# A two-layer RWKV-7 and Conformer backbone on one core: latent chains get PSUM banks, state and tiles of their own, and the next pair's chain is written right behind its merge

## The chip, the cores and the metric

The kernel runs on one core of a Trainium2 chip. The metric is the device time of one execution in microseconds (us); lower is better.

## What is computed

The input is a stream of 512 latent tokens and a prefix of 256 context tokens, each of width 1024. The first layer (below) runs an RWKV-7 mixer in both directions over context and latents, with 16 heads of 64, beside a gated short convolution; both go through one output projection. The second layer is a Conformer convolution on the latents alone.

```python
def wkv_scan(S0, r, decay, k, v, kk, a, reverse):
    def step(S, inp):
        sa = jnp.einsum("bhvk,bhk->bhv", S, -kk_t)
        S = (S * w_t[:, :, None, :] + sa[..., None] * (kk_t * a_t)[:, :, None, :]
             + v_t[..., None] * k_t[:, :, None, :])
        return S, jnp.einsum("bhvk,bhk->bhv", S, r_t)
...
    yac, S_f, S_b = rwkv_seq(rwkv_prep(hc, rc, kc, vc, *rw), zero, zero, ...)
    ya, _, _ = rwkv_seq(rwkv_prep(h, r, k, v, *rw), S_f, S_b, r_k, lnx_w, lnx_b, True)
    yb = bg * dwconv(cg * xb, sc_w, seg_len)
    y = jnp.concatenate([ya * jax.nn.silu(za), yb * jax.nn.silu(zb)], axis=-1) @ w_out
```

## The kernel before

**Tiling.** The recurrence is taken in chunks of 64 tokens (4 of the context, 8 of the latents) and in 8 pairs of heads. A pair's work falls into steps: `prep_lat`, `light` and `heavy` make the products within the chunks (AR, BK, and E, the masked matrices); `solve` inverts the triangular blocks on VectorE, with a transpose of Nt into X (L737) and 31 times a product (xtmp, L743) and a sum (Y, L745); `merge` joins the inverted blocks and writes them into E; the chain then goes over the chunks in sequence. `finish` normalises a pair's outputs and turns them (po), and `conv_branch` makes the short convolution of the same columns, with four projections in the order cg, xb, bg, zb; the last of them (tile pzb) gates its result.

**The chain.** `chain_lat(st, i)` is one of 8 steps, forward and backward direction (z = 0, 1) at once. A step is a line of dependent pieces: matmuls of the state H and of earlier values into zo; ScalarE copies the sum to Zs (L865); matmuls with E into uh; ScalarE copies them to UV (L872); matmuls with BKt into the same bank uh; VectorE makes the new state Hl from it (L879); ScalarE scales it for the next step (HPl, L833). The step's outputs collect in bank on (tile onl) and are evicted at the step's end, by ScalarE in steps 0 to 3 (L888) and by an addition on VectorE in steps 4 to 7 (L891), into tile O. PSUM tiles zo, on, po and the merge's mg rotate over three banks (`ps_zo`: two with tag zo, and uh1); uh of all chains is one bank.

**The order.** Each engine takes its instructions in its own queue, in order. The queues are laid out when the program is built: a list scheduler takes what is ready by its planned times, and among these what was written first. The written order is the loop over 12 stages (from L1049): stages 0 to 3 run the context chains, 4 to 11 the chains of latent pairs 0 to 7. A latent stage writes its own chain, and then by the letters of `STAGE[2]` ("OSPLMHFC"): O (po of the next stage), S (solve of the next), P and L (prep and light of the one after), M (merge of the next), H (heavy of the one after), F (projection fills, and finish of its own), C (conv_branch, one pair behind the chain's count: stage 10 writes convolution 7 and stage 11 only the last chain and its finish).

**The end of the layer.** Behind convolution 7 the pool of the right side is closed and the out-projection's pool opened in its space, so the loads of wr (the rows of w_out) and yr wait until the last gate projection has read its operands. `outproj` makes 384 matmuls (tiles o) for the first half of the tokens: for each of 16 row blocks, ScalarE casts wr to wh and VectorE subtracts to wl (`hilo`), and three products each are taken. Block 8 has its weights in early tiles (we8h, we8l). The matmuls of out-projection stand behind chain 7 in the written order.

## Time and profile before

| | us |
|---|---|
| median of 3 runs | 1387.38 (1385.10 to 1389.39) |
| profiled execution, its time | 1384.0 |
| profiled execution, its span | 1382.2 |
| TensorE matmuls, busy | 1319.8 (95%) |
| VectorE, busy | 986.4 (71%) |
| ScalarE, busy | 744.4 (54%) |
| clock granted to TensorE, mean share | 0.992 |

The span is the time from the first to the last instruction of the profile. In profile lines PE is TensorE's matmuls, PEld its weight loads (which overlap them), DVE VectorE, ACT ScalarE, POOL GpSimd, and SPq the queue from which SyncE issues transfers. Starts and durations are in us from the span's start; `x` counts instructions, and `<-` in square brackets names what ended a wait. Tiles are named by the program, with their numbers left out: Hl is the state of a latent chain, ARl a latent AR.

| in the profile of before | us |
|---|---|
| first latent chain's state update | from 484.5 |
| last latent chain's first matmul | 871.4 |
| last latent chain's last output | 901.9 |
| layer 1's first out-projection matmul | 872.0 |

### The profile page before, as it was taken

To read this page: it belongs to the slowest core of one execution; us is meant where nothing else is said; L and a number is where in the kernel's file an instruction comes from. 1 tells how busy PE (TensorE), PEld (TensorE's weight loads), DVE (VectorE), ACT (ScalarE), POOL (GpSimd) and SP (SyncE) were. 2 spreads that over 40 slices of the span, in tenths; PEclk is the share of its full clock that TensorE was granted. 3 is DMA by queue.
4 is the path that set the end of the run, shared out by engine and by line. 5 is a ranking of instruction groups with operands and counts; after the bars stand their busy time and mean duration, and the time that the engine had idled before them with its cause. 6 is when DMAs were issued, how large, how long until landed. Compare 5 with 4: busy or idle time off the path is not lost.

```text
span 1382.2 us, 29703 instructions
## 1 busy us (share of the span) xinstructions
PE 1319.8 (95%) x11925; PEld 975.1 (71%) x11925; DVE 986.4 (71%) x2304; ACT 744.4 (54%) x1509; POOL 127.7 (9%) x263
## 2 busy tenths in 40 slices
PE   6999999999998999999999989999999999999998
PEld 2657777777666766666666666677777787788886
DVE  5857879867999499999999998458653653644323
ACT  6546476555765476675756755547742432554222
POOL 4142200001101010101101000010000000000000
PEclk9999999999999999999999999999999999999999
DMA  9865522222323322223222221578621321133232
GB/s 334 272 215 198 161 62 75 92 75 77 96 86 88 97 76 73 78 66 86 77 72 78 76 72 48 187 264 284 203 70 53 122 74 49 62 116 98 92 99 84
DMA packets 139754, 158.54 MB, mean 115 GB/s; under 512 B 15503, under 2 KB 104223, under 8 KB 139497
## 3 DMA queue, kind: packets, MB, share of 16 engines
q1 hardware_dynamic: 123152, 106.47, 24.9%
q0 software_dynamic: 15856, 49.12, 10.9%
q8 instruction: 93, 1.52, 0.5%
q10 hardware_dynamic: 608, 1.06, 0.2%
q14 instruction: 45, 0.37, 0.1%
HBM read 138.33 MB, written 18.28 MB: 113 GB/s over the span
## 4 chain that ended last, share of the span: by engine, by line
PE 46%; DVE 12%; ACT 7%; issue 4%; DMA 4%; POOL 0%; SPq 0%; DVEq 0%; ACTq 0%; POOLq 0%
PE pu L57 12%; PE pz L57 6%; PE f L57 6%; PE pxb L57 3%; PE pcg L57 3%; PE uh L57 3%; PE o L57 2%; DVE E L686 2%; DMA wr<-in_ev_w_out_dram 2%; PE pzb L57 1%; PE zol L57 1%; PE onl L57 1%; PE px L57 1%; PE pc L57 1%; DVE Yl L745 1%
## 5 line engine op out<-in xcount | busy, mean ns | idle before, releaser
L57 PE MATMUL o<-wh,y 128*128 128x512 f32 x248 | 79.8, 396 | 0.0
L743 DVE TENSOR_TENSOR xtmpl<-Xl,Yl 128x126 f32<-128x126 f32 (+22 forms) x248 | 62.3, 251 | 3.1
L745 DVE TENSOR_TENSOR Yl<-Yl,xtmpl 128x126 f32<-128x126 f32 (+22 forms) x248 | 62.2, 251 | 2.9
L1281 ACT CAST ah<-a 64x512 fp32r<-64x512 f32 x32 | 19.8, 618 | 74.8 <-DVE a L1276 74.4
L57 PEld LDWEIGHTS uh<-UV,BKt 128*64 128x64 f32 x704 | 26.4, 136 | 37.6 <-ACT UV L872 27.8
L57 PEld LDWEIGHTS o<-wh,y 128*128 128x128 f32 x248 | 46.2, 188 | 9.5
L57 PE MATMUL pal<-ARl,BKl 64*128 64x128 f32 x512 | 44.5, 295 | 8.7 <-DVE E L686 7.3
L57 PE MATMUL o<-wl,y 128*128 128x512 f32 x124 | 49.7, 401 | 2.3 <-DVE wl L130 2.3
L872 ACT COPY UV<-uh 64x128 f32<-64x128 f32 x128 | 33.3, 260 | 28.9 <-PE uh L57 26.6
L57 PEld LDWEIGHTS pal<-ARl,BKl 64*128 64x128 f32 x512 | 35.3, 191 | 18.8 <-issue 11.1
L130 DVE TENSOR_TENSOR wl<-wr,wh 128x1024 fp32r<-128x1024 f32 x28 | 34.2, 1223 | 19.1 <-ACT wh L129 19.0
L1276 DVE TENSOR_TENSOR a<-pu,a 128x512 f32<-128x512 f32 x16 | 11.0, 691 | 50.0 <-PE pu L57 47.7
L57 PE MATMUL uh<-UV,BKt 128*64 128x64 f32 x704 | 36.5, 232 | 8.7 <-ACT UV L872 4.5
L686 DVE TENSOR_TENSOR E<-pal,maskE 128x512 f32<-128x512 f32 x64 | 42.9, 684 | 0.3
L1233 DVE SCALAR_TENSOR_TENSOR pr<-px,dbe,What 119x512 f32<-119x512 f32 x32 | 22.6, 746 | 26.6 <-PE px L57 26.6
L129 ACT CAST wh<-wr 128x1024 fp32r<-128x1024 f32 x28 | 29.6, 1056 | 19.3 <-DMA wr<-in_ev_w_out_dram 10.1
L57 PEld LDWEIGHTS uh<-Ol,E 64*64 64x64 f32 x512 | 20.3, 133 | 25.8 <-ACT Ol L865 23.6
L879 DVE SCALAR_TENSOR_TENSOR Hl<-uh,PCl,HPl 128x64 f32<-128x64 f32 x112 | 26.2, 276 | 13.7 <-PE uh L57 5.2
L833 ACT ACTIVATE HPl<-Hl,PCl 128x64 f32<-128x64 f32 x96 | 28.1, 340 | 11.0 <-DVE Hl L879 9.8
L745 DVE TENSOR_TENSOR Yc<-Yc,xtmpc 128x126 f32<-128x126 f32 (+22 forms) x124 | 31.5, 254 | 3.1
L743 DVE TENSOR_TENSOR xtmpc<-Xc,Yc 128x126 f32<-128x126 f32 (+22 forms) x124 | 31.5, 254 | 3.0
L57 PEld LDWEIGHTS zol<-Hl,ARl 64*64 64x64 f32 x448 | 18.0, 134 | 21.0 <-DVE xtmpl L743 5.4
(1002 smaller groups left out, 4284.1 us busy)
## 6 DMA issues: line engine op xcount, KB each, us to landing
wr<-in_ev_w_out_dram SPq DMA_DIRECT2D x28, 512.0 KB, 5.2
mwr<-in_mod_w_dram POOLq DMA_DIRECT2D x28, 256.0 KB, 4.2
wrv<-in_ev_w_in_dram SPq DMA_DIRECT2D x16, 256.0 KB, 2.9
ectx<-in_mod_w_dram POOLq DMA_DIRECT2D x16, 256.0 KB, 4.4
wrr<-in_ev_w_in_dram SPq DMA_DIRECT2D x16, 256.0 KB, 2.9
wrza<-in_ev_w_in_dram SPq DMA_DIRECT2D x16, 256.0 KB, 2.8
wrcg<-in_ev_w_in_dram SPq DMA_DIRECT2D x16, 256.0 KB, 2.9
wrxb<-in_ev_w_in_dram SPq DMA_DIRECT2D x16, 256.0 KB, 2.9
```

The source lines that it names most:

```text
L57: env["pe"] = T.matmul(o, lhsT, rhs, start=start, stop=stop)
L129: S.copy(hi, raw)
L130: env["lo"].tensor_tensor(out=lo, in0=raw, in1=hi, op=ALU.subtract)
L686: st["ev"].append(V.tensor_tensor(out=E[:, h, z * NLAT + c0 : z * NLAT + c0 + m, :], in0=pas[h], in1=maskE[:, z * (1 + h) : z * (1 + h) + ...
L743: V.tensor_tensor(out=tv, in0=X[:, :i, i : i + 1].to_broadcast([P, i, m]), in1=Y[:, i : i + 1, c0:].to_broadcast([P, i, m]), op=ALU.mult)
L745: V.tensor_tensor(out=Y[:, :i, c0:], in0=Y[:, :i, c0:], in1=tv, op=ALU.add)
L833: S.activation(t[:, z, :], H[:, z, :], AF.Copy, scale=st["PC"][z][:, i : i + 1])
L872: u_ = S.copy(UV[ZR[1 - h], i : 2 * nch - i : 2 * nch - 1 - 2 * i, ZR[h]], uh[ZR[1 - h], 0:2, :])
L879: h_ = V.scalar_tensor_tensor(out=Hn[:, z, :], in0=uh[:, 2 + z, :], scalar=PC[z][:, i : i + 1], in1=HP[:, z, :], op0=ALU.mult, op1=ALU.add)
L1233: V.scalar_tensor_tensor(out=pr[s][:NPROD], in0=px[s][:NPROD], scalar=dbe[:, 0:1], in1=What[:, n * 512 : n * 512 + 512], op0=ALU.add, op1= ...
L1276: V.tensor_tensor(out=a, in0=pp[1], in1=a, op=ALU.mult)
L1281: S.copy(ahl[s][hr], a[hr])
```

## The change

Every latent chain gets two banks by its pair's parity: X (uh0 or uh1) for the sums that were in zo, and Y (one of the two zo tiles, now named zy0 and zy1) for uh, the state update and the outputs. H and HP are halves of fixed tiles. The two directions' AR lie in one tile, and Zs and the outputs overwrite the chunks of AR that are used up, so the tile O goes. A step's outputs are no longer computed and evicted in the step itself: `outs(i, H)` keeps them, and step i+1 takes the first four matmuls between its own, the other four behind its copy Zs, and then evicts, ahead of its matmuls into Y. `merge` of a latent pair writes into solve's tiles X and Y from pair 1 on. `finish` turns the outputs in the pair's bank Y. In the written order, only stage 4 writes its own chain; a latent stage writes the next pair's chain (new letter X) right behind the next pair's merge.

```diff
-STAGE = ("KLSMVHvF", "OPLSMHF", "OSPLMHFC")
+STAGE = ("KLSMVHvF", "OPLSMHF", "OSMXPLHFC")
...
-    def ps_zo(name):
-        flip["zo"] = (flip["zo"] + 1) % 3
-        return ps.tile([P, 512], F32, tag="uh1" if flip["zo"] == 2 else "zo", name=name, bufs=1 if flip["zo"] == 2 else 2)
...
-    NBUF = {"tmp": 3, "bon": 3, "AR": 6, "BK": 2, "BKt": 4, "UV": 2, "E": 2, "PC0": 4, "PC1": 4, "rnq": 2,
+    NBUF = {"tmp": 3, "bon": 3, "AR": 3, "BK": 2, "BKt": 4, "UV": 2, "E": 2, "PC0": 4, "PC1": 4, "rnq": 2,
...
+        if st["lat"] and st["p"]:
+            Xt, Yt = st["XY"]
+            R1, R2, Gs = (t.rearrange("p (a b) -> p a b", b=32) for t in (Xt[:, 0:512], Xt[:, 512:], Yt))
...
-        pg = px = ps_zo("mg" + nm)
+        pg = px = uhs[1 - st["p"] % 2] if st["lat"] else uhs[1]
...
         if i == 0:
+            par = p % 2
+            if not lat2:
+                lat2["y"] = [ps.tile([P, 512], F32, tag="zo", name=f"zy{x}", bufs=2) for x in range(2)]
+                lat2["h"] = [w(t, f"{t}l{x}") for x, t in enumerate(("H", "H", "HP"))]
+            st["py"] = lat2["y"][par]
+            st["xy"] = ch3(uhs[1 - par]), ch3(lat2["y"][par])
+            *st["hn"], st["hp"] = [t[:, par * P : par * P + P].rearrange("p (z x) -> p z x", z=2) for t in lat2["h"]]
             st["HP"] = scale_H(st, st["H"], 0)
-            st["O"] = ch3(w("O", f"O{nm}"))
+            st["go"] = pinned()
...
+        def outs(i, H):
+            cs = (i, nch - 1 - i)
+            oc = (4, 5) if i < nch // 2 else (5, 4)
+            first = [(lambda h=h, z=z: go(Y[ZR[h], oc[z], :], AR[z][ZR[h], cs[z], CH:], H[ZR[h], z, :], z == 1, False))
+                     for z in (1, 0) for h in (1, 0)]
+            then = [(lambda h=h, z=z: go(Y[ZR[h], oc[z], :], E[:, h, z * nch + cs[z], CH:],
+                                         UV[:, z * nch + cs[z], ZR[h]], False, z == 1)) for h, z in hz]
+
+            def evict():
+                if i < nch // 2:
+                    S.copy(Q[:, 2 * i + 1 : 32 - 2 * i : 30 - 4 * i, :], Y[:, 4:6, :])
+                else:
+                    o = Q[:, 15 - 2 * i : 18 + 2 * i : 2 + 4 * i, :]
+                    V.tensor_tensor(out=o, in0=Y[:, 4:6, :], in1=o, op=ALU.add)
+
+            return first, then, evict
...
-        zo, on = st["zo"], ch3(ps_zo(f"on{nm}_{i}"))
+        first, then, evict = st.get("outs") or ([], [], lambda: None)
         for z in (1, 0):
             for h in range(2):
-                m0_ = cmm(zo[ZR[1 - h], z, :], AR[z][ZR[h], cs[z], 0:CH], H[ZR[h], z, :], False, z == 0)
-                cmm(on[ZR[1 - h], oc[z], :], AR[z][ZR[1 - h], cs[z], CH:], H[ZR[1 - h], z, :], z == 1, False)
+                m0_ = go(X[ZR[1 - h], z, :], AR[z][ZR[h], cs[z], 0:CH], H[ZR[h], z, :], False, z == 0)
+                if first:
+                    first.pop(0)()
...
-        S.copy(Zs, zo[:, 0:2, :])
+        Zs = Q[:, 2 * i : 31 - 2 * i : 30 - 4 * i, :]
+        S.copy(Zs, X[:, 0:2, :])
+        closing([], then, evict)
         ahead = values(i + 1) if i < nch - 1 else []
         for h, z in hz:
-            cmm(uh[ZR[1 - h], z, :], E[ZR[1 - h], h, z * nch + cs[z], 0:CH], Zs[ZR[1 - h], z, :])
+            go(Y[ZR[1 - h], z, :], E[ZR[1 - h], h, z * nch + cs[z], 0:CH], Zs[ZR[1 - h], z, :])
...
+        st["outs"] = outs(i, H)
...
-        else:
+        elif s == 4:
             for i in range(NLAT):
                 chain_lat(st, i)
...
+            elif x == "X":
+                for i in range(NLAT):
+                    chain_lat(sts[s + 1], i)
```

What this moves in the queues is shown at three places.

**TensorE at the end of convolution 7.** pzb7 is the gate projection of the last convolution; o01 and its like are out-projection. Before, the last pzb7 rows and the first step of chain 7 (zol7, onl7) read:

```order
L57 MATMUL pzb7_10982<-hlh1_447,whzb71_10977 128x512
L57 MATMUL pzb7_10982<-hll1_448,whzb71_10977 128x512
L57 MATMUL pzb7_10982<-hlh1_447,wlzb71_10978 128x512
L57 MATMUL zol7_0_11021<-UV110_4903,E110_4904 64x64 x4
L57 MATMUL zol7_0_11021<-h0_7_9897,ARl71_9989 64x64
L57 MATMUL onl7_0_11026<-h0_7_9897,ARl71_9989 64x64
L57 MATMUL zol7_0_11021<-h0_7_9897,ARl71_9989 64x64
L57 MATMUL onl7_0_11026<-h0_7_9897,ARl71_9989 64x64
L57 MATMUL zol7_0_11021<-h0_7_9897,ARl70_9959 64x64
L57 MATMUL onl7_0_11026<-h0_7_9897,ARl70_9959 64x64
L57 MATMUL zol7_0_11021<-h0_7_9897,ARl70_9959 64x64
L57 MATMUL onl7_0_11026<-h0_7_9897,ARl70_9959 64x64
L57 MATMUL o01_11335<-we8h_11340,ye8_11338 128x512
L57 MATMUL o01_11335<-we8l_11341,ye8_11338 128x512
```

After, uh0 and zy1 are chain 7's banks X and Y, and these are the last pzb7 rows and the rest of that step's matmuls up to the first row of out-projection:

```order
L57 MATMUL zy1_5340<-UV110_4884,E110_4885 64x64 x4
L57 MATMUL pzb7_10958<-hlh1_443,whzb71_10953 128x512
L57 MATMUL pzb7_10958<-hll1_444,whzb71_10953 128x512
L57 MATMUL pzb7_10958<-hlh1_443,wlzb71_10954 128x512
L57 MATMUL zy1_5340<-ARl7_10051,E110_4885 64x64
L57 MATMUL uh0_125<-UV110_4884,E110_4885 64x64
L57 MATMUL zy1_5340<-ARl7_10051,E110_4885 64x64
L57 MATMUL uh0_125<-UV110_4884,E110_4885 64x64
L57 MATMUL zy1_5340<-ARl7_10051,E110_4885 64x64
L57 MATMUL uh0_125<-UV110_4884,E110_4885 64x64
L57 MATMUL zy1_5340<-ARl7_10051,E110_4885 64x64
L57 MATMUL uh0_125<-UV110_4884,E110_4885 64x64
L57 MATMUL o01_11031<-we8_11036,ye8_11034 128x512 x2
```

The last pzb7 stood ahead of the first matmul of chain 7 and stands now in its sixth step (step 5); out-projection began in the first step and begins now in the sixth.

**VectorE around the start of solve 7.** The transpose into Xl7 is solve 7's first instruction; orq5 and bonl5 belong to the finish of pair 5 and yb6 to convolution 6. Before:

```order
L954 TENSOR_TENSOR yb6_10302<-pbg6_10318,yb6_10302 128x512
L502 TENSOR_TENSOR orq5_10188<-orq5_10188 128x8
L130 TENSOR_TENSOR wlcg70_10853<-wrcg70_10851,whcg70_10852 128x512
L503 TENSOR_TENSOR orq5_10188<-orq5_10188 128x8
L504 SCALAR_TENSOR_TENSOR orq5_10188<-orq5_10188 128x8
L911 TENSOR_TENSOR Ol5_9551<-Ol5_9551,orq5_10188 128x512
L686 TENSOR_TENSOR E110_4904<-pal7000_10110,maskE_107 128x512
L686 TENSOR_TENSOR E110_4904<-pal7001_10111,maskE_107 128x512
L920 SCALAR_TENSOR_TENSOR bonl5_8260<-po5_10203,hcol_77,bonl5_8260 128x512
L921 SCALAR_TENSOR_TENSOR bonl5_8260<-bonl5_8260,hcol_77,gz5_10220 128x512
L737 STREAM_TRANSPOSE Xl7_10668<-Nt_111 128x32x32
L743 TENSOR_TENSOR xtmpl7_10670<-Xl7_10668,Yl7_10669 128x31
```

After, at the same place, with Hl0, the first state update of chain 6:

```order
L942 TENSOR_TENSOR ARl5_8449<-ARl5_8449,orq5_10201 128x2x4x64
L915 SCALAR_TENSOR_TENSOR Hl0_5341<-zy0_5339,PCl60_9243,HPl2_5343 128x64
L915 SCALAR_TENSOR_TENSOR Hl0_5341<-zy0_5339,PCl61_9272,HPl2_5343 128x64
L737 STREAM_TRANSPOSE Xl7_10401<-Nt_111 128x32x32
L743 TENSOR_TENSOR xtmpl7_10403<-Xl7_10401,Yl7_10402 128x31
L745 TENSOR_TENSOR Yl7_10402<-Yl7_10402,xtmpl7_10403 128x31
L743 TENSOR_TENSOR xtmpl7_10403<-Xl7_10401,Yl7_10402 128x30
```

and a few rows on:

```order
L915 SCALAR_TENSOR_TENSOR Hl1_5342<-zy0_5339,PCl60_9243,HPl2_5343 128x64
L915 SCALAR_TENSOR_TENSOR Hl1_5342<-zy0_5339,PCl61_9272,HPl2_5343 128x64
L951 SCALAR_TENSOR_TENSOR bonl5_8426<-zy1_5340,hcol_77,bonl5_8426 128x512
L743 TENSOR_TENSOR xtmpl7_10403<-Xl7_10401,Yl7_10402 128x81
L952 SCALAR_TENSOR_TENSOR bonl5_8426<-bonl5_8426,hcol_77,gz5_10232 128x512
L745 TENSOR_TENSOR Yl7_10402<-Yl7_10402,xtmpl7_10403 128x27x3
L743 TENSOR_TENSOR xtmpl7_10403<-Xl7_10401,Yl7_10402 128x78
L745 TENSOR_TENSOR Yl7_10402<-Yl7_10402,xtmpl7_10403 128x26x3
L130 TENSOR_TENSOR we8_11036<-wre8_11037,we8_11036 128x1024
L985 TENSOR_TENSOR yb6_10314<-pbg6_10330,yb6_10314 128x512
```

The first update of chain 6 stood 22 rows behind the transpose of solve 7 and stands now just ahead of it; bonl5 and yb6, which stood ahead, now stand among the solve's operations.

**ScalarE where out-projection's first weights are cast.** y0_9 and wh0_9 are the casts of the first block of yr and wr; UV110 is the chain's copy. Before, from the last cast of convolution 7's weights into the second step of chain 7:

```order
L129 CAST whzb71_10977<-wrzb71_10976 128x512 [waits DMAHW7_49,PE_49]
L898 ACTIVATE gzb7_11007<-pzb7_10982 128x512 [waits PE_49]
L865 COPY Ol7_11020<-zol7_0_11021 128x128 [waits DVE_49,PE_49,Activation_49]
L872 COPY UV110_4903<-uh0_125 64x2x64 [waits PE_49]
L872 COPY UV110_4903<-uh0_125 64x2x64
L129 CAST y0_9_11361<-yr0_9_11362 128x256 [waits DMAHW0_49]
L888 COPY Ol7_11020<-onl7_0_11026 128x2x64 [waits PE_49]
L833 ACTIVATE HPl7_1_11054<-Hl7_0_11051,PCl70_9952 128x64 [waits DVE_49]
L833 ACTIVATE HPl7_1_11054<-Hl7_0_11051,PCl71_9981 128x64
L865 COPY Ol7_11020<-zol7_1_11036 128x128 [waits PE_49]
L129 CAST wh0_9_11367<-wr0_9_11366 128x1024 [waits DMAHW1_49]
L872 COPY UV110_4903<-uh0_125 64x2x64 [waits PE_49]
```

After, from the Zs copy of step 5 (ARl7) of chain 7:

```order
L899 COPY ARl7_10051<-uh0_125 128x2x64 [waits PE_49]
L929 ACTIVATE gzb7_10983<-pzb7_10958 128x512 [waits PE_49]
L907 COPY UV110_4884<-zy1_5340 64x2x64 [waits DVE_49,PE_49]
L907 COPY UV110_4884<-zy1_5340 64x2x64
L837 ACTIVATE HPl2_5343<-Hl1_5342,PCl70_10044 128x64 [waits DVE_49]
L837 ACTIVATE HPl2_5343<-Hl1_5342,PCl71_10073 128x64 [waits DVE_49,Activation_49]
L129 CAST y0_9_11056<-yr0_9_11057 128x256 [waits DMAHW0_49]
L899 COPY ARl7_10051<-uh0_125 128x2x64 [waits PE_49]
L129 CAST wh0_9_11062<-wr0_9_11061 128x1024 [waits DMAHW1_49]
L907 COPY UV110_4884<-zy1_5340 64x2x64 [waits DVE_49,PE_49]
```

The cast wh0_9 stood ahead of the UV copies of step 1 and stands now ahead of those of step 6; the gate gzb7 stood ahead of the chain and stands in its step 5.

More of the change, by code (lines that the diff above doesn't have):

```diff
@@ L161 @@
     l0, rs = ExitStack(), ExitStack()
-    flip = {"mm": 0, "at": 0, "zo": 0}
+    flip = {"mm": 0, "at": 0}
     I32 = mybir.dt.int32
@@ L249, in start @@
         dft = w("xtmp", "dft")[:31, :NPROD]
-        tokt = [w("AR", f"tok{j}") for j in range(6)]
+        tokt = [t[:, D * j : D * j + D] for t in [w("AR", f"tok{j}") for j in range(3)] for j in range(2)]
         for j in range(6):
@@ L855, in chain_lat, with closing @@
+        def closing(first, then, evict):
+            for f in first + then:
+                f()
+            evict()
         if i == 0:
-            for go in values(0):
-                go()
-        zo, on = st["zo"], ch3(ps_zo(f"on{nm}_{i}"))
+            for f in values(0):
+                f()
+        first, then, evict = st.get("outs") or ([], [], lambda: None)
         for z in (1, 0):
             for h in range(2):
-                m0_ = cmm(zo[ZR[1 - h], z, :], AR[z][ZR[h], cs[z], 0:CH], H[ZR[h], z, :], False, z == 0)
-                cmm(on[ZR[1 - h], oc[z], :], AR[z][ZR[1 - h], cs[z], CH:], H[ZR[1 - h], z, :], z == 1, False)
+                m0_ = go(X[ZR[1 - h], z, :], AR[z][ZR[h], cs[z], 0:CH], H[ZR[h], z, :], False, z == 0)
+                if first:
+                    first.pop(0)()
@@ L871, in chain_lat @@
         for h in range(2):
-            u_ = S.copy(UV[ZR[1 - h], i : 2 * nch - i : 2 * nch - 1 - 2 * i, ZR[h]], uh[ZR[1 - h], 0:2, :])
+            u_ = S.copy(UV[ZR[1 - h], i : 2 * nch - i : 2 * nch - 1 - 2 * i, ZR[h]], Y[ZR[1 - h], 0:2, :])
         h_ = None
+        st["outs"] = outs(i, H)
         if i < nch - 1:
             for h, z in hz[::-1]:
-                cmm(uh[ZR[h], 2 + z, :], BKt[z][:, cs[z], ZR[h]], UV[:, z * nch + cs[z], ZR[h]])
-            Hn = w("H", f"H{nm}_{i}")[:, 0:P].rearrange("p (z x) -> p z x", z=2)
+                go(Y[ZR[h], 2 + z, :], BKt[z][:, cs[z], ZR[h]], UV[:, z * nch + cs[z], ZR[h]])
+            Hn = st["hn"][i % 2]
             for z in range(2):
-                h_ = V.scalar_tensor_tensor(out=Hn[:, z, :], in0=uh[:, 2 + z, :],
+                h_ = V.scalar_tensor_tensor(out=Hn[:, z, :], in0=Y[:, 2 + z, :],
                                             scalar=PC[z][:, i : i + 1], in1=HP[:, z, :], op0=ALU.mult, op1=ALU.add)
@@ L883, in chain_lat @@
                 st["HP"] = scale_H(st, Hn, i + 1)
+        else:
+            closing(*st["outs"])
         st.setdefault("anc", []).append([x.ins for x in (m0_, u_, h_) if x is not None])
-        for h, z in hz:
-            cmm(on[ZR[h], oc[z], :], E[:, h, z * nch + cs[z], CH:], UV[:, z * nch + cs[z], ZR[h]], False, z == 1)
-        if i < nch // 2:
-            S.copy(O[:, i : nch - i : nch - 1 - 2 * i, :], on[:, 2:4, :])
-        else:
-            o = O[:, nch - 1 - i : i + 1 : 2 * i + 1 - nch, :]
-            V.tensor_tensor(out=o, in0=on[:, 2:4, :], in1=o, op=ALU.add)
     def gate(p, cb, nm):
@@ L910, in finish @@
         rsqrt(rw[:, 8:16], rw[:, 0:8], rw[:, 16:24])
-        V.tensor_tensor(out=O3, in0=O3, in1=rw[:, 8:16].unsqueeze(2).to_broadcast([P, 8, CH]), op=ALU.mult)
-        po = ps_zo(f"po{p}")
+        V.tensor_tensor(out=O3, in0=O3, in1=rw[:, 8:16].rearrange("p (g c) -> p g c", g=2).unsqueeze(3)
+                        .to_broadcast([P, 2, 4, CH]), op=ALU.mult)
         go = pinned()
@@ L1123, in early @@
         else:
-            hl = [w(tag, f"we{k}{x}", F32R) for x in "hl"]
+            t = w(tag, f"we{k}", F32R)
+            hl = [t[:, x * D : x * D + D] for x in range(2)]
         return y, yr, [w("BK", f"wre{k}")[:, 0:D]] + hl
```

48 lines of the change are left out of this document (25 added, 23 removed).

## The prediction

> **What bounds the kernel now.** I read the shares of busy time first, then a table of windows over the latent stages, then the chain of waits at their end.
>
> ```profile
> PE 1319.8 (95%) x11925; PEld 975.1 (71%) x11925; DVE 986.4 (71%) x2304; ACT 744.4 (54%) x1509; POOL 127.7 (9%) x263
> ```
>
> TensorE looks like the bound throughout. By windows (columns: us, then busy time of PE, PEld, DVE, ACT, POOL with instruction counts, the clock, the DMA share) there are two regimes:
>
> ```profile
> 480.00:536.00 56.00, 53.53 (x722) 36.78 (x720) 52.45 (x156) 37.33 (x90) 6.75 (x12) 1.00 0.27 78
> ...
> 654.00:711.00 57.00, 54.58 (x778) 37.86 (x776) 53.29 (x155) 37.41 (x90) 6.73 (x12) 1.00 0.27 78
> ...
> 768.00:825.00 57.00, 54.23 (x772) 37.25 (x770) 53.17 (x152) 35.17 (x85) 3.49 (x7) 1.00 0.25 77
> 880.00:900.00 20.00, 19.63 (x283) 12.50 (x281) 10.23 (x23) 12.38 (x37) 0.00 (x0) 1.00 0.64 217
> 920.00:940.00 20.00, 20.00 (x89) 16.55 (x89) 8.69 (x16) 10.57 (x19) 0.00 (x0) 1.00 0.96 339
> ```
>
> Up to about 825 a stage takes 57 us and VectorE is busy for some 53 of them. TensorE's 54 are small, widely spaced matmuls (x778 in 57 us; its weight loads fill only 38). VectorE sets this pace. From about 860 VectorE is half idle and TensorE sets the end. This is the chain of waits at the border:
>
> ```profile
> 865.99 5.48 PE pzb L57 x24
> 871.49 0.34 SPq L126
> ...
> 872.36 6.10 DMA wr<-in_ev_w_out_dram
> 878.50 0.93 issue
> ...
> 901.84 7.02 PE o L57 x30
> 908.88 1.15 PE po L57 x32
> 910.02 4.99 PE o L57 x21
> ```
>
> The gates of the last convolution branch (pzb) end at 871.47; only then are the out-projection's weights (wr) fetched, and from there TensorE runs almost without a gap. So the tail ends when TensorE's fixed work is done, plus whatever it idles.
>
> **The change, part by part.** The PE, ACT and DVE instructions do the same arithmetic in the same number; what moves is their place. Up to the first latent chain (about 480 us) the order is practically the old one: 0.
>
> *1. Two chains side by side.* In the new order every chain k still ends before chain k+1 begins; nothing overlaps. A chain is moved ahead by some 10 us of VectorE work, to before the next solve. Overlap itself is worth 0.
>
> *2. VectorE in the steady stages.* The solve is pairs of dependent operations. Alone, and with another between:
>
> ```profile
> 705.70 0.21 DVE L743 TENSOR_TENSOR xtmpl<-Xl,Yl 128x31 f32<-128x31 f32 x1
> 705.94 0.21 DVE L745 TENSOR_TENSOR Yl<-Yl,xtmpl 128x31 f32<-128x31 f32 x1
> ...
> 685.99 0.17 DVE L743 TENSOR_TENSOR xtmpl<-Xl,Yl 128x16 f32<-128x16 f32 x1
> 686.07 0.69 DVE L686 TENSOR_TENSOR E<-pal,maskE 128x512 f32<-128x512 f32 x1
> ```
>
> The dependent one starts 0.03 us after the record before it ends, the independent one 0.09 before: 0.12 us a neighbourhood. The new order has 22 fewer of them in solves 1 to 6 (65 for 87), since the chain's H updates and output adds fall between the solve's operations: 22 x 0.12 = **2.6 us saved**. Here the Trainium skill speaks differently: "VectorE: DVE Perf Modes", section "The DRAIN you can't avoid", measures the same time for eight copies with a semaphore after each and after the last alone. By that this term would be 0 and the sum below 8.9; the section allows an operation that is not held to start earlier, which is what the rows above show.
>
> What VectorE leaves idle in these stages is small. The sum from 480 to 820, and its waits there (us in total, times, the longest):
>
> ```profile
> 480.00:820.00 340.00, 321.48 (x4578) 222.56 (x4577) 320.41 (x934) 219.43 (x525) 36.41 (x65) 1.00 0.26 75
> DVE Ol L891 <- PE onl L57: 4.5, 6, 1.2
> ...
> DVE Hl L879 <- PE uh L57: 1.8, 5, 0.5
> DVE Hl L879 <- ACT sg L590: 1.7, 4, 0.7
> ```
>
> Idle are 340 - 320.4 = 19.6 us, and 8.0 of them are waits of the chain's own operations (4.5 + 1.8 + 1.7).
>
> Whether these waits shrink (the chain starts earlier and has its own banks) or grow (less other VectorE work stands between the end of a solve and the first H update behind its merge: some 11 us in the new order, about what merge and first step take by themselves, where 13 to 27 stood) no row shows. Bounds: 19.6 us less, all of the idle time, and 13 us more (the evictions below). I take 0: the balance of 53 busy in 57 stays the nearest row.
>
> *3. Outputs in the chain's own bank.* In the new code a step's outputs share bank Y with uh and the H update, and are evicted in the next step ahead of the uh matmuls, which wait for it. Before, onl had a bank out of three and stood off the chain. The price is a copy or an add on the path of each step:
>
> ```profile
> L888 ACT COPY Ol<-onl 128x128 f32<-128x128 f32 x32 | 8.3, 260 | 13.6 <-PE onl L57 13.6
> L891 DVE TENSOR_TENSOR Ol<-onl,Ol 128x128 f32<-128x128 f32 x32 | 9.1, 283 | 8.3 <-PE onl L57 8.3
> ```
>
> Seven evictions ahead of uh: 4 x 0.26 + 3 x 0.28 = 1.9 us per chain at most, and 0 where TensorE's fillers or VectorE's queue end last. In the steady stages the chain isn't the last to end, so 0; if it were, 7 x 1.9 = 13. In chain 7 I count 1.0, the four copies before the place that matters below. The Trainium skill, "PSUM — Partial Sum Buffer", its summary table, advises to read PSUM in a different bank from the one that the running matmuls write and to guard by bank; merging three uses into one bank goes against it. By it the sum below would be 12 us higher, all 13 in place of 1.0; no row shows that yet.
>
> *4. The tail.* This is the largest term. In the old order the last pbg and pzb matmuls run in a block before chain 7, and chain 7's gaps are filled with the out-projection:
>
> ```profile
> 820.18 2.04 DVE L737 STREAM_TRANSPOSE Xl<-Nt 128x1024 f32<-128x1024 f32 x1 [0.38 <-ACT Nt L705]
> 851.01 1.12 DVE L751 STREAM_TRANSPOSE kdml<-Yl 128x512 f32<-128x512 f32 x1
> 861.97 0.69 DVE L770 COPY E<-mgl 32x512 f32<-32x512 f32 x1
> 874.33 0.48 DVE L879 SCALAR_TENSOR_TENSOR Hl<-uh,PCl,HPl 128x64 f32<-128x64 f32 x2 [0.79 <-PE uh L57]
> 898.53 0.48 DVE L879 SCALAR_TENSOR_TENSOR Hl<-uh,PCl,HPl 128x64 f32<-128x64 f32 x2 [1.44 <-ACT UV L872]
> ```
> ```profile
> 872.00:901.84 29.84, 20.17 (x61) 1.00 0.68 222
> ```
>
> Solve 7 begins at 820.2 and ends at 851.0, merge 7 takes 11.7 (to 862.7), the pzb block ends at 871.47, chain 7 makes a step in (898.53 - 874.33)/6 = 4.03 us, and 61 of the 384 out-projection matmuls (12 of them with we8, whose weights are there early) are done at 901.84, by the last row (a window that counts the out-projection's matmuls alone). In the new order chain 7 follows merge 7 at once, pbg and pzb are its fillers up to its sixth step, and only the 12 we8 matmuls follow there. The wr loads still wait for the last pzb.
>
> - Solve 7 starts at 820.2 - 2.6 = 817.6. Between its first and last operation about 3.3 us of VectorE work is added (two bonl of pair 5's finish, yb and a cast, which stood ahead of it, 0.6 to 0.75 each). It had 30.8 us with waits; I add half: 32.5, end 850.1.
> - Merge 11.7. ACT's cast whzb, for 16 pxb matmuls behind po6, now stands ahead of the merge's E copy. Between 0 and 16 x 0.225 = 3.6 (0.225 from the 89 matmuls in 20.00 us above) I take half, 1.7. Chain 7 starts at 863.5.
> - The last pzb stands behind 5.3 of its steps. TensorE is full there in either kernel: 61 fillers in 7.5 steps before are 8.1 a step, now 48 (24 pbg, 24 pzb) in 5.3 steps 9.1, so a step gets 0.225 longer, 4.25. 863.5 + 5.3 x 4.25 + 1.0 (evictions) = 887.0, where it was 871.47.
> - The first matmul with a wr weight follows 6.9 after the last pzb, and the wh cast ends after 5.3:
>
> ```profile
> 871.49 0.34 SPq L126 DMA_DIRECT2D wr<-in_ev_w_out_dram  x1
> 875.71 1.05 ACT L129 CAST wh<-wr 128x1024 fp32r<-128x1024 f32 x1
> 878.33 0.39 PE L57 MATMUL o<-wh,y 128*128 128x512 f32 x1
> 878.00:884.00 6.00, 5.63 (x69) 1.00 1.02 381
> ```
>
>   (The last row counts TensorE alone: 5.63 us busy of 6.) So the out-projection begins in earnest at 887.0 + 6.9 = 893.9. ACT's queue has that cast ahead of the UV copy of the seventh step, so this step waits until 887.0 + 5.3 = 892.3 too and the chain can't use the gap. At 893.9 the chain has 1.3 steps left.
> - At 901.84 before, 384 - 61 = 323 matmuls are left. In the new kernel 372 are left at 893.9. The 49 between cost 49 x 0.225 = 11.0. A chain step costs TensorE (29.84 - 61 x 0.225)/7.5 = 2.15 us, 1.3 of them 2.8. The start of the stream has 0.4 idle (5.63 of 6.00). 323 are left at 893.9 + 11.0 + 2.8 + 0.4 = 908.1: **6.3 us late**. The 2.6 us saved are in this already; the tail alone gives back 8.9.
>
> The block of pzb that went is no loss by itself; idle TensorE behind it is, since the cover (out-projection in chain 7's gaps) is gone.
>
> Sum: -2.6 + 8.9 = +6.3. The profiled execution took 1384.0 (span 1382.2), so 1390.3 by it. The three runs' median is 1387.38, 3.4 above it; I put the difference on the median: **1394 us**.
>
> **The rivals.** With G the gain up to solve 7's start, the sum is 8.9 - G. 0.3%, 4.2 us, is about what a measurement here can tell from no change.
>
> *A, forecast:* G = 2.6, 1394. For it: the wr loads' gate and the place of pzb are certain from the order.
>
> *B, half of the chain's waits go:* G = 2.6 + 4.0 = 6.6, the sum +2.3, 1390. For it: an output's add no longer waits for its own step's matmuls, since it stands a step later. Against: less other work stands before each chain's first H update.
>
> *C, the other side, VectorE's idle time closes:* its queue is in order, so an add or an H update that comes up too early stops solve and prep behind it. If the chain's 8.0 us of waits went and half of the other 11.6, G would be 2.6 + 8.0 + 5.8 = 16.4, the sum -7.5, and the time 1380. It is faster by over 0.3% once G is over 13.1, that is once 10.5 of the 19.6 idle us are gone. Against: the chain's operations stand in the same in-order queue as before, and the next wait takes over.
>
> *D, evictions on the path:* if the chain binds its stage, +1 us a stage (half of 1.9, six stages) on top of A: 1400; all of it: 1407.
>
> *E, the change does not do what it says:* no overlap, as found under 1. That by itself is no time; it is contained in A. If TensorE interleaved two chains after all, VectorE's 53 us per stage would remain, and the time A's.
>
> **How the numbers follow.** A 0.50 (of which 0.05 within 0.3%, a smaller stall), B 0.20 (all within 0.3%), C 0.15 (faster), D 0.15 (slower). Faster 0.15, same 0.25, slower 0.60. The likeliest case has 1394, its own range 1389 to 1399. The range must reach C's 1380 and most of D: **1380 to 1405**; beyond are the full 13 us of D and a C in which still more idle time goes.
>
> **What would show it.** In the changed profile: solve 7's transpose near 818 (A), 804 (C) or 824 (D); the last pzb near 887; the first o with wh near 894 with PE idle some 5 us in the 20 before it; the stages' distance 56 to 57 us; VectorE's chain waits from 480 to 820 in sum near 8. The prediction fails if the wr loads come before the last pzb, or if the gap ahead of them is filled with other matmuls.

## The result, and the profile after

The changed kernel takes **1396.1 us** (median of 5 runs, 1395.26 to 1399.55) against 1387.38 (5 runs, 1381.33 to 1389.39): ratio 1.0076, 95% interval 1.0049 to 1.0103. It is slower, by 8.7 us of the medians, where 6.6 were forecast. The profiled execution has a span of 1395.3 us against 1382.2: 13.1 more to account for (that of before lay 3.4 us under its median, that of the changed kernel, 1397.06, lies 1.0 over).

The profile page's row of busy times and the window over the steady stages, for the changed kernel (the same rows of before stand in the prediction):

```profile
PE 1332.4 (95%) x11925; PEld 986.0 (71%) x11925; DVE 984.8 (71%) x2304; ACT 744.3 (53%) x1509; POOL 127.4 (9%) x263
...
480.00:820.00 340.00, 320.64 (x4375) 222.54 (x4373) 307.74 (x908) 213.53 (x516) 35.87 (x64) 0.99 0.24 71
```

VectorE's work is the same in sum, but it did 12.7 us less of it from 480 to 820 (307.74 for 320.41): it idles for 32.3 us there and no longer for 19.6. So the loss sits in the stages for which I had forecast a gain of 2.6 us. TensorE counts 12.6 us more of busy time for the same 11925 matmuls; in a dense row matmuls overlap (those of pzb take 0.39 us and start 0.23 us apart), so this number depends on how they stand (the 192 of pzb count 51.0 us before and 56.8 now, the 384 of out-projection 96.3 and 91.3), and I don't read it as more work. These rows of VectorE's timeline (start, duration) give the milestones of the end: solve 7's transpose, merge 7 (now in tile Xl), the first and the last state update of chain 7.

```profile
831.53 2.00 DVE L737 STREAM_TRANSPOSE Xl<-Nt 128x1024 f32<-128x1024 f32 x1
...
865.34 1.19 DVE L755 STREAM_TRANSPOSE Xl<-Yl 128x512 f32<-128x512 f32 x1
876.85 0.48 DVE L915 SCALAR_TENSOR_TENSOR Hl<-zy,PCl,HPl 128x64 f32<-128x64 f32 x2 [0.63 <-PE zy L57]
...
902.88 0.67 DVE L915 SCALAR_TENSOR_TENSOR Hl<-zy,PCl,HPl 128x64 f32<-128x64 f32 x2 [0.25 <-PE zy L57]
```

All solves are done when merge 7 starts, so this is the mark that I compare: 865.34 for 851.01, 14.3 us late. From there to the end it takes 530.0 us (1395.3 - 865.3) for 531.2: **nothing is lost behind merge 7**. The order moves this mark a little: 2839 matmuls are left behind it where 2910 were, 1.0 us less of busy time; TensorE idles there for 9.4 us, for 9.7 before. Of the 14.3, 4.1 were there at the first latent state update (488.6 for 484.5), and 10.2 came in the stages between. These are the windows between the two marks, before and then after:

```profile
484.54:851.01 366.47, 346.21 (x4913) 238.40 (x4913) 343.41 (x1017) 235.56 (x568) 36.96 (x67) 1.00 0.26 75
```
```profile
488.61:865.34 376.73, 355.75 (x5001) 247.12 (x5000) 342.93 (x1023) 236.77 (x577) 37.52 (x68) 1.00 0.24 72
```

VectorE's idle time grew by 10.7 us, from 23.1 to 33.8, and TensorE's by 0.7.

The chain of waits around the out-projection's start:

```profile
895.26 0.91 PE pzb L57 x3
896.16 0.02 issue
896.18 4.12 DMA wr<-in_ev_w_out_dram
900.30 0.02 issue
900.33 1.06 ACT wh L129
```

The last pzb and the first wr load did move, to 896.2 from 871.5, and further than forecast (887). But TensorE does not idle ahead of them:

```profile
880.00:900.00 20.00, 19.81 (x265) 12.62 (x266) 5.19 (x16) 8.59 (x30) 0.54 (x1) 1.00 0.17 48
900.00:920.00 20.00, 19.88 (x170) 14.88 (x169) 15.91 (x34) 11.32 (x20) 0.54 (x1) 1.00 0.86 296
```

19.81 of 20 us are busy where I expected a gap of some 5. Before, 61 out-projection matmuls were done 50.83 us behind merge 7 (851.01 to 901.84); the forecast had the same count 58.0 us behind it (908.1 - 850.1). A window of 50.83 us in the changed kernel, which counts these matmuls alone, has 62:

```profile
865.34:916.17 50.83, 16.09 (x62) 1.00 0.40 133
```

And a chain takes longer: state updates of one chain stand 4.55 us apart (mean over chains 0 to 6, each from its first and last of seven updates) where they stood 4.04.

### The profile page after: what moved, and what is told of

The parts are those of the page before. It is cut to its first block, busy times and chain, and to the rows that moved or that the text cites. A ratio compares the mean times of both kernels' runs of the same rounds, so it can differ in the third digit from the quotient of the medians.

```text
span 1395.3 us, 29738 instructions
## 1 busy us (share of the span) xinstructions
PE 1332.4 (95%) x11925; PEld 986.0 (71%) x11925; DVE 984.8 (71%) x2304; ACT 744.3 (53%) x1509; POOL 127.4 (9%) x263
## 4 chain that ended last, share of the span: by engine, by line
PE 50%; DVE 9%; issue 7%; ACT 5%; DMA 3%; POOL 1%; DVEq 0%; POOLq 0%; ACTq 0%; SPq 0%
PE pu L57 10%; PE pz L57 6%; PE f L57 6%; PE zy L57 5%; PE o L57 4%; PE pcg L57 3%; PE pxb L57 3%; PE uh L57 2%; PE pzb L57 2%; PE pbg L57 2%; DVE E L686 1%; PE px L57 1%; PE plr L57 1%; PE pc L57 1%; DMA wr<-in_ev_w_out_dram 1%
## 5 line engine op out<-in xcount | busy, mean ns | idle before, releaser
L907 ACT COPY UV<-zy 64x128 f32<-64x128 f32 x128 | 33.4, 261 | 35.4 <-PE zy L57 34.1
L57 PEld LDWEIGHTS pal<-ARl,BKl 64*128 64x128 f32 x512 | 34.5, 192 | 21.1 <-issue 11.5
L686 DVE TENSOR_TENSOR E<-pal,maskE 128x512 f32<-128x512 f32 x64 | 43.5, 683 | 2.6 <-PE zy L57 2.3
L915 DVE SCALAR_TENSOR_TENSOR Hl<-zy,PCl,HPl 128x64 f32<-128x64 f32 x112 | 26.7, 278 | 21.7 <-PE zy L57 9.0
L1268 DVE SCALAR_TENSOR_TENSOR pr<-px,dbe,What 119x512 f32<-119x512 f32 x32 | 22.6, 746 | 26.6 <-PE px L57 26.6
L57 PEld LDWEIGHTS zy<-ARl,E 64*64 64x64 f32 x512 | 20.4, 133 | 24.3 <-ACT ARl L876 10.9
L57 PEld LDWEIGHTS zy<-UV,BKt 128*64 128x64 f32 x448 | 17.6, 136 | 25.5 <-ACT UV L907 23.6
L57 PE MATMUL uh<-UV,E 64*64 64x64 f32 x512 | 29.0, 230 | 3.8 <-DVE E L774 3.8
L57 PEld LDWEIGHTS uh<-Hl,ARl 64*64 64x64 f32 x448 | 17.8, 133 | 19.9 <-DVE Yl L745 5.1
```

The lines of the kernel that those rows point to most:

```text
L57: env["pe"] = T.matmul(o, lhsT, rhs, start=start, stop=stop)
L686: st["ev"].append(V.tensor_tensor(out=E[:, h, z * NLAT + c0 : z * NLAT + c0 + m, :], in0=pas[h], in1=maskE[:, z * (1 + h) : z * (1 + h) + ...
L907: u_ = S.copy(UV[ZR[1 - h], i : 2 * nch - i : 2 * nch - 1 - 2 * i, ZR[h]], Y[ZR[1 - h], 0:2, :])
L915: h_ = V.scalar_tensor_tensor(out=Hn[:, z, :], in0=Y[:, 2 + z, :], scalar=PC[z][:, i : i + 1], in1=HP[:, z, :], op0=ALU.mult, op1=ALU.add)
L1268: V.scalar_tensor_tensor(out=pr[s][:NPROD], in0=px[s][:NPROD], scalar=dbe[:, 0:1], in1=What[:, n * 512 : n * 512 + 512], op0=ALU.add, op1= ...
```

## The experiments

Besides the theory of the prediction (T, the tail) there were four more: E, the eviction of the outputs from the chain's own bank stands in the chain's way; S, the start itself is later; M, merge in solve's tiles holds back the next solve; A, the AR tiles are held longer. All kernels were timed against the kernel of before; its median was 1385 to 1387 in these runs, and the text quotes each ratio with its interval.

### Only the last chain back behind convolution 7

```diff
-        elif s == 4:
+        elif s in (4, 11):
...
-            elif x == "X":
+            elif x == "X" and s < 10:
```

> The changed kernel, with one thing undone: only the last chain (pair 7) is again written behind convolution 7, as before the change; chains 1 to 6 stay right behind their merges, and banks, tiles and deferred outputs stay too. Theory T (tail: the wr loads wait for the last pzb matmul, which stands in step 5 of chain 7): pzb ends ahead of chain 7 as before, the first wr load goes out near 877 instead of 896, and 8 to 10 us come back: 1386 to 1388. Theory E (the evictions in the chain's own bank lengthen every chain): only chain 7's neighbourhood changes, 1394 to 1397. Theory S (a later start: the changed profile is 3 us behind at 112 us already): 3 us stay lost in either case, so with T 1388 to 1390.

Measured: 1399.64 us, ratio 1.0095 (1.0067 to 1.0124). Nothing came back. Merge 7 starts at 863.8, as late as in the changed kernel. The last pzb did go back ahead of chain 7, and the first wr load out at 882.7 for 896.2; yet from merge 7 to the end it takes 532.7 us (1396.5 - 863.8) for 530.0. T falls as the explanation.

### The old written order, with the new banks, tiles and deferred outputs

```diff
-STAGE = ("KLSMVHvF", "OPLSMHF", "OSMXPLHFC")
+STAGE = ("KLSMVHvF", "OPLSMHF", "OSPLMHFC")
...
-        elif s == 4:
+        else:
```

> The changed kernel with the written order of before in all stages (every stage writes its own chain at its start), so that only the new banks, tiles and deferred outputs are left. T: as fast as before, 1385 to 1389, since the tail has the order of before. E: every chain is longer by 7 x 0.27 = 1.9 us, and where it is last in its stage this shows: up to 13 us, 1394 to 1400; the state updates of a chain stand 4.4 us apart instead of 4.1. S: 3 us over before at 112 us in the profile.

Measured: 1398.7 us, ratio 1.0092 (1.0062 to 1.0123); state updates 4.42 us apart; the first of them at 483.1. As E said. The new written order, one half of the change, is not needed for the loss: with it, 1396.1, without it, 1398.7, and their intervals overlap.

### Outputs in another bank, in the changed order

The eight matmuls and the eviction of the outputs go to the bank X of the other parity instead of Y (`ob`), four places in `outs`.

```diff
+            st["ob"] = ch3(uhs[par])
...
-            first = [(lambda h=h, z=z: go(Y[ZR[h], oc[z], :], AR[z][ZR[h], cs[z], CH:], H[ZR[h], z, :], z == 1, False))
+            first = [(lambda h=h, z=z: go(ob[ZR[h], oc[z], :], AR[z][ZR[h], cs[z], CH:], H[ZR[h], z, :], z == 1, False))
```

> The changed kernel, but the deferred outputs collect in the bank X of the other parity instead of in Y with uh and the state update, so that their eviction doesn't stand ahead of the uh matmuls. E: the state updates go back from 4.4 to 4.1 us apart, and with them up to 10 us: 1386 to 1390. T: the planned order puts the last pzb matmul in the second step of chain 7 here, 4 steps earlier than in the changed kernel, so some 4 x 4.2 = 17 us earlier ahead of the wr loads: most of the 9 us come back too, 1387 to 1390. The times don't tell the two apart, the spacing of the state updates in stages 5 to 9 and the place of the first wr load do.

Measured: 1416.85 us, ratio 1.0208 (1.0180 to 1.0237). A miss on the time, though the spacing fell as E said: 3.88, 3.92, 4.04 and 3.71 us in the first four chains (4.56, 3.74 and 4.35 in the next three). Then something else happens. Two windows of ten us (PE's busy time is the first value behind the window's length, the clock the value before the last two):

```profile
760.00:770.00 10.00, 2.42 (x68) 2.35 (x69) 9.79 (x22) 3.66 (x8) 3.44 (x6) 0.59 0.32 93
770.00:780.00 10.00, 9.58 (x123) 7.04 (x119) 7.28 (x18) 3.44 (x8) 0.57 (x1) 0.56 0.38 108
```

and from the waits between 755 and 775:

```profile
PEld uh L57 <- DVE Xl L756: 8.3, 1, 8.3
```

TensorE stands 8.3 us at a merge's matmul, whose transpose is queued behind the next pair's preparation on VectorE, and the granted clock falls to 0.59 and 0.56. The other bank is also the next merge's; that this meeting brought about the stand isn't shown, since what ended the wait is the transpose. The variant doesn't test E by its time.

### The same, with outputs in their own step

The first four output matmuls are interleaved with the step's own, the other four and the eviction come at its end, as before the change; the bank stays the other one.

```diff
-        first, then, evict = st.get("outs") or ([], [], lambda: None)
+        first, then, evict = outs(i, H)
...
-        else:
-            closing(*st["outs"])
+        closing([], then, evict)
```

> As the run with the other bank, but the outputs are also computed and evicted in their own step again, as before the change; chains still stand right behind their merges. E: spacing of the state updates 4.1 us, as before. T: the planned order has all pzb matmuls ahead of chain 7 here, so the first wr load goes out some 20 us earlier than in the changed kernel and the tail costs nothing: 1385 to 1388, though every chain is still written early. If the early chain itself (and not where the pzb matmuls stand) were what costs, it would stay near 1396.

Measured: 1435.79 us, ratio 1.0335 (1.0291 to 1.0380), against both theories. The pzb matmuls ahead of chain 7 did not help, and state updates stood 4.1 to 6.2 us apart. The clock was 0.62 in the window 750 to 800 and 0.63 from 850 to 900. What is longer in a step lies ahead of its Zs copy: 1.93 us from the state update to it, for 1.26 in before (means as in the table further below). There the next step's first output matmuls stand between the chain's own; that they wait for the eviction from the one bank that they now have, in place of a rotation of three, is my reading.

### The old order, only tiles and banks of the change

The two edits above (outputs in the other bank, and in their own step) on the old written order, and merge in its old tiles:

```diff
-        if st["lat"] and st["p"]:
-            Xt, Yt = st["XY"]
-            R1, R2, Gs = (t.rearrange("p (a b) -> p a b", b=32) for t in (Xt[:, 0:512], Xt[:, 512:], Yt))
-        else:
-            R1, R2, Gs = (w(t, f"{t}m{nm}")[:, 0:512].rearrange("p (a b) -> p a b", b=32) for t in ("kd", "a", "P"))
+        R1, R2, Gs = (w(t, f"{t}m{nm}")[:, 0:512].rearrange("p (a b) -> p a b", b=32) for t in ("kd", "a", "P"))
```

> Only tiles and banks of the change: written order of before, outputs made and evicted in their own step, in the bank X of the other parity; merge uses the tiles of before; left of the change are the paired AR tiles that also hold Zs and outputs, the fixed halves of H and HP, and banks by parity. Three theories on where the 10 us go that all four runs so far lost ahead of solve 7's start: E (evictions in the chain's bank Y stretch each step from 4.05 to 4.5 us), M (merge in solve's tiles X and Y holds back the next solve's transpose until the merge is done), A (the AR tiles are held until a pair's outputs are turned, so the preparation of a later pair waits). E and M: 1384 to 1390. A: 1394 to 1400.

Measured: 1403.87 us, ratio 1.0129 (1.0105 to 1.0152), with 4.35 us between state updates. That is above even the range of A; but the run further below with the same tiles at 1384.75, which differs from this one by the deferral alone, excludes A. What is left is the single bank, which the next step's first outputs find not yet evicted. The place of the loss fits (1.74 us from the state update to the Zs copy, for 1.24 with the outputs deferred); that these outputs wait for the eviction is argued.

### The old order, merge in its old tiles, outputs deferred in bank Y

> Written order of before, merge in the tiles of before, but deferred outputs in the chain's bank Y as in the change. E: the state updates of a chain stay 4.4 to 4.5 us apart and the time stays at 1394 to 1399 (the old order with merge in solve's tiles took 1398.7). M: 1385 to 1390, with solve 2's transpose back near 528 instead of 534 to 539.

Measured: 1398.7 us, ratio 1.0097 (1.0073 to 1.0121), 4.44 us between updates. The old order with merge in solve's tiles took 1398.7 as well: M falls, in this order.

### The changed order, merge in its old tiles

> The changed kernel with one thing undone: merge writes into the tiles of before (kd, a, P) instead of solve's X and Y. M: the transposes of solves 2 to 4 start ahead of the merge's end again, and 7 to 10 us come back: 1386 to 1389. E: 1394 to 1398, with state updates 4.5 us apart.

Measured: 1468.03 us, ratio 1.0594 (1.0561 to 1.0628). Far from either theory. kd, a and P are also the next pair's preparation's, and that now comes behind the chain:

```profile
480.00:820.00 340.00, 295.27 (x3840) 212.34 (x3838) 275.29 (x759) 186.72 (x446) 30.99 (x56) 0.91 0.22 65
```

VectorE idles for 64.7 of 340 us and the stages take 71.5. So merge in solve's tiles is what makes the new written order bearable, not a cost. The state updates stand 4.19 us apart here, where E had 4.5: the shared bank alone doesn't set a step's length, though the piece that holds the eviction stays long (0.68 us from the Zs copy to the matmuls behind the eviction, for 0.26 in before).

### The old order, outputs deferred in the other bank

This differs from the run in bank Y by the bank alone (the four places of `ob`).

> As the tiles-only run, but the outputs are deferred by a step, still in the other bank. E: the evictions don't stand in the way of the uh matmuls, 3.9 to 4.1 us between state updates and 1384 to 1390. If deferring itself costs (its four matmuls now stand ahead of the next step's uh matmuls), 1392 to 1398 with 4.3 us or more between them.

Measured: **1384.75 us**, ratio 0.9991 (0.9976 to 1.0006), 3.88 us between updates. All the loss is gone, with the paired AR tiles, the halves of H and the deferral still in place. So A falls, and deferring costs nothing. The pair of runs that differ by a bank, 1398.7 and 1384.75, says 14.0 us for it. The first and the last update of chain 5, in bank Y and then in the other bank:

```profile
781.84 0.43 DVE L911 SCALAR_TENSOR_TENSOR Hl<-zy,PCl,HPl 128x64 f32<-128x64 f32 x2
...
808.40 0.48 DVE L911 SCALAR_TENSOR_TENSOR Hl<-zy,PCl,HPl 128x64 f32<-128x64 f32 x2 [0.30 <-PE zy L57]
```
```profile
774.86 0.43 DVE L913 SCALAR_TENSOR_TENSOR Hl<-zy,PCl,HPl 128x64 f32<-128x64 f32 x2
...
797.71 0.47 DVE L913 SCALAR_TENSOR_TENSOR Hl<-zy,PCl,HPl 128x64 f32<-128x64 f32 x2
```

26.6 us for six steps, and 22.9: 0.6 us a step. Merge 7 starts at 859.5 in the one and at 851.0 in the other: 8.5 of the 13.6 us between the two profiles lie ahead of it, and 5.1 behind it, where 44 matmuls more are left to do.

In step 2 of this chain one sees where the time goes: the Zs copy (L895 and L897), the eviction (L872 and L874) and the first of the matmuls with E into Y, again in bank Y and then in the other bank:

```profile
787.03 0.25 ACT L895 COPY ARl<-uh 128x128 f32<-128x128 f32 x1
...
787.34 0.27 ACT L872 COPY ARl<-zy 128x128 f32<-128x128 f32 x1
...
788.11 0.27 PE L57 MATMUL zy<-ARl,E 64*64 64x64 f32 x1
```
```profile
779.36 0.24 ACT L897 COPY ARl<-uh 128x128 f32<-128x128 f32 x1
...
779.98 0.27 PE L57 MATMUL zy<-ARl,E 64*64 64x64 f32 x1
...
780.09 0.26 ACT L874 COPY ARl<-uh 128x128 f32<-128x128 f32 x1
```

In bank Y these matmuls stand behind the eviction in all 42 steps (1 to 6 of chains 0 to 6); in the other bank they mostly don't. The means over these steps, from the rows of the profiles (a state update counted from the start of its second instruction):

| us | state update to the start of the Zs copy | end of the Zs copy to the first matmul with E |
|---|---|---|
| before | 1.26 | 0.26 |
| changed kernel | 1.38 | 0.83 |
| old order, deferred, bank Y | 1.30 | 0.78 |
| old order, deferred, other bank | 1.24 | 0.25 |
| old order, own step, other bank | 1.74 | 0.32 |
| changed order, own step, other bank | 1.93 | 0.36 |
| before, outputs in the bank of uh | 2.06 | 0.34 |

Of the 0.56 us by which the two spacings differ, 0.53 lie in the one piece that holds the eviction, and in the changed kernel this piece has grown by as much (0.57); in the variants of the changed order with the other bank and deferred outputs it has 0.25 and 0.20. So the mechanism of E is shown in both orders, its price in time only in the old one.

### The changed order, outputs in the other bank, merge in bank Y

The edits of `ob`, and one for merge:

```diff
-        pg = px = uhs[1 - st["p"] % 2] if st["lat"] else uhs[1]
+        pg = px = (lat2["y"][st["p"] % 2] if lat2 else uhs[1 - st["p"] % 2]) if st["lat"] else uhs[1]
```

> The changed kernel (each chain right behind its merge) with the outputs in the bank X of the other parity, and merge in the pair's bank Y, so that the outputs of one chain and the next merge don't meet in a bank, as they did in the first run with the other bank (there TensorE stood 8.3 us at the merge and its clock fell to 0.56). Theory E (a step of the chain waits for the eviction from its own bank): state updates 3.9 to 4.1 us apart, and 10 to 14 us come back: 1382 to 1387. If the early chain costs by itself (TensorE's queue then holds merge and chain ahead of the next pair's preparation, and stands at them), 1395 or more, with PE idle for several us at a time and a clock under 0.95 in some stages.

Measured: 1400.04 us, ratio 1.0105 (1.0080 to 1.0130), with 3.91 us between updates. The bank is out of the way and the time did not come back. From the old order with the other bank at 1384.75 this kernel differs by the written order, and by the tiles and the bank of merge; the tiles were no cost in the old order. So here the early chain costs, or the bank that merge has with it. Solve 5's transpose stands at 710.8 (703.7 in before), solve 6's at 775.9 and solve 7's at 838.9, so the last two stages take 65 and 63 us. In one of them:

```profile
800.00:820.00 20.00, 12.51 (x121) 9.89 (x121) 19.86 (x54) 10.12 (x20) 0.54 (x1) 0.92 0.11 30
820.00:840.00 20.00, 19.12 (x336) 14.74 (x336) 13.07 (x33) 10.92 (x32) 1.07 (x2) 0.82 0.22 62
```

First VectorE is full and TensorE stands 7.5 us, of which 5.5 are one wait of a matmul of the next pair's preparation (pal) for VectorE's E (L686); then VectorE idles for 7, and the clock is 0.82. As I read it, the chain is over too early to fill the gaps of the work that follows; no run tests that reading.

### The fastest variant, with the last chain early

```diff
-        else:
+        elif s < 11:
...
-        for x in STAGE[(s >= 2) + (s >= 4)]:
+        for x in ("OSMXFC" if s == 10 else STAGE[(s >= 2) + (s >= 4)]):
```

> The fastest variant so far (written order of before, outputs deferred in the other bank, merge in the tiles of before, 1384.75), with only the last chain written right behind merge 7, ahead of convolution 7. The tail term of the prediction: the last pzb stands in step 6 of chain 7, the wr loads go out 10 to 15 us later and 5 to 9 us are lost: 1390 to 1394. Against it, TensorE's work being only exchanged (pzb fills chain 7 in place of out-projection, and no gap opens): 1381 to 1386, as writing chain 7 early took 1396.1 and late 1399.6 in the changed kernel.

Measured: 1385.12 us, ratio 1.0005 (0.9985 to 1.0025): the tail term alone, with nothing else in the way, is worth 0 within the interval (-2.1 to +3.5 us against before). The first wr load does go out 13.4 us later (without the early chain, and with it):

```profile
871.63 0.34 SPq L126 DMA_DIRECT2D wr<-in_ev_w_out_dram  x1
```
```profile
884.99 0.34 SPq L126 DMA_DIRECT2D wr<-in_ev_w_out_dram  x1
...
875.00:900.00 25.00, 25.00 (x309) 1.00 0.54 178
```

The second fence's last row is a window that counts TensorE alone: it is busy for 25.00 of 25 us behind the late gate. By 950 us, 255 out-projection matmuls are done for 263, but merge 7 started 2.0 us later in that execution (853.0 for 851.0); in the 99 us behind merge 7, 264 are done in either. The late gate itself leaves no trace.

### The kernel of before, with outputs in the bank of uh

The eight output matmuls of a step move to its end, so that their group is closed by itself, and go to uh's bank.

```diff
-        zo, on = st["zo"], ch3(ps_zo(f"on{nm}_{i}"))
+        zo, on = st["zo"], uh
...
-                cmm(on[ZR[1 - h], oc[z], :], AR[z][ZR[1 - h], cs[z], CH:], H[ZR[1 - h], z, :], z == 1, False)
...
+        for z in (1, 0):
+            for h in (1, 0):
+                cmm(on[ZR[h], oc[z], :], AR[z][ZR[h], cs[z], CH:], H[ZR[h], z, :], z == 1, False)
```

> The kernel of before with one thing added: the outputs of a step collect in the bank of uh and are evicted from it at the step's end, in place of a bank of the rotation. All their eight matmuls stand at the step's end. E: the next step's uh matmuls wait for the eviction, state updates 4.4 to 4.8 us apart instead of 4.05, and 10 to 15 us lost: 1395 to 1401. If the shared bank is no cost and something else of the change is, 1385 to 1390.

Measured: 1420.8 us, ratio 1.0253 (1.0227 to 1.0279), with 4.74 us between updates: some 20 us more than E expected, in E's direction, but not at E's place. By the table above the piece between the Zs copy and uh has 0.34 us for 0.26, and the piece ahead of the Zs copy 2.06 for 1.26: there the eight output matmuls, moved to the step's end, stand ahead of the next step's sums (zo). So this run prices the moved matmuls together with the bank, and not the wait that E is about.

### The kernel of before once more

> The kernel of before, unchanged, profiled once more, to see how far the start scatters between executions: the first latent state update stood at 484.5 us in its profile and at 488.6 in the changed kernel's, at 483 to 492 in the other variants, though nothing ahead of it was changed in some of them. If this is scatter, it lies 1 to 5 us away from 484.5 here, while the stages behind it keep their length (merge 7 starts 364 to 369 us after it). If the early part of the change costs 4 us by itself, it stands within 1 us of 484.5.

Measured: 1384.3 us, one execution (a second one of the same kernel took 1390.7). The first latent update stands at 486.58, 2.0 us later than in the first profile, and merge 7 at 851.13, where it stood at 851.01. That is scatter, with 364.5 us between the two marks for 366.5: the start moves by some us from one execution to the next, and part of it is made up on the way. So the 4.1 us at 488.6 are not shown to be the change's; variants with the changed order had 486.1 to 488.6 there, those with the old order 483.1 to 491.6. The granted clock goes along: what it misses of 1.00 in the windows of ten us ahead of 480 adds up to 8.6 us in the first profile of before, 10.4 in this one and 12.1 in the changed kernel's, where the first update stands at 484.5, 486.6 and 488.6. Which brings about which isn't shown.

## Why the prediction came out where it did

The time, its sign and its range held: 1394 forecast, 1396.1 measured. The **way there did not**. Against the profile of before, the terms are:

| | forecast, us | measured, us |
|---|---|---|
| up to the first latent update | 0 | +4.1, scatter of the start at least in part |
| first latent update to merge 7 | -2.6, and +1.7 in solve 7 | +10.2 |
| merge 7 to the end | +7.2 | -1.2 |
| span | +6.3 | +13.1 |

- *Two chains side by side, 0.* Right: in the changed kernel each chain's last state update stands ahead of the next chain's first (857.8 and 876.9 for the last two).
- *VectorE in the steady stages.* Failed. I took its idle time as unchanged since 53 of 57 us were busy. The 2.6 us of dependent neighbours may have been saved, but the idle time rose by 12.7 from 480 to 820, and no run tells the 2.6 apart. Solve 7's transpose, near 818 by A and 824 by D, stood at 831.5. The chain's own waits on VectorE hardly changed: 9.2 us before (the forecast's 8.0 left out three rows of its view, in which Hl waits for whbg, Pl and iPl) and 9.8 after. Most of the growth stands at other operations, 5.3 us of it at wlcg, which waits for ScalarE's cast whcg; how the longer chain brings this about no run shows.
- *The outputs in the chain's own bank.* This is the step that failed most: "In the steady stages the chain isn't the last to end, so 0". At 0.27 us an eviction it was also priced too low: a step grew by 0.51 (4.04 to 4.55), and by 0.56 in the pair that differs by the bank alone (3.88 to 4.44). The waits of the weight loads (484 to 820) name the Zs copy (L865) before, and in the changed kernel the eviction copy (L876), which ends later:

```profile
PEld uh L57 <- ACT UV L872: 20.9, 41, 1.0
PEld uh L57 <- ACT Ol L865: 15.9, 40, 0.8
```
```profile
PEld zy L57 <- ACT UV L907: 20.5, 46, 0.9
PEld zy L57 <- ACT ARl L876: 8.0, 18, 0.9
```

  These waits are shorter in sum, so they say which copy ends last and not what it costs; the cost is in the table, 0.26 to 0.83 us in that piece of a step. In the old order it comes to what rival D had said at its full price (13 us): 14.0. That the two are alike is luck: D counted 1.9 us a chain, where a chain grew by 3.4 from its first to its last update (6 x 0.56) and not all of that reached the time. D had 0.15. The Trainium skill's advice in "PSUM — Partial Sum Buffer", summary table, is to read a bank other than the one that matmuls write. The pair agrees with it, 1384.75 for 1398.7 us, and I had set it aside without a row against it.
- *The tail, +8.9.* Failed, on the sizes of its pieces. From merge 7 to the first state update of chain 7 I had 16.3 us (850.1 to 866.4, which is 863.5 and the 2.9 from a chain's first matmul to its first update), it took 11.5; from there to the last pzb 20.6, it took 19.3; from there to the first matmul with wh 6.9, it took 5.6 (901.76). These are 7.4 us of the 8.4 by which the part behind merge 7 came out below its +7.2. The largest is merge 7 itself: 7.5 us (865.34 to 872.83) where I had 13.4, for the 11.7 of before have the end of chain 6 in them (its last update at 854.58). The mechanism, too, was not there: TensorE's work was exchanged, pbg and pzb for out-projection, and no idle time opened. The run with the last chain early shows this with nothing else changed.

So two wrong terms of opposite sign, and a start 4.1 us late, gave a sum near the right one: that the time lies close to the forecast is luck. What the loss of the changed kernel is by part is settled for its banks in the old order (14.0 us). In its own order it is not: the three variants that freed the bank there lost as much or more, and in two of them TensorE stands for over 7 us within 20, so the shared bank's part of the 10.2 us there is argued from the state updates' spacing and from the table, and not shown by a time.

No variant beat the kernel of before: the best, at 1384.75, is the same within its interval.

## What to carry to other kernels

Before a step's output is put into a bank of the dependent chain, count its eviction as part of every step, even where another engine looks like the bound: VectorE was busy for 93% of a stage, and yet its idle time could grow from 23.1 to 33.8 us between the same two marks. Where one engine is full and its work is only exchanged, as TensorE was here, a load that goes out later need not cost anything until the engine really stands; look for that idle time before pricing the gate. And a sum that comes out right proves none of its terms: compare at a mark which the order hardly moves, and count the work left behind it.
